# Convolution with max-pooling on one core: the last image pair's rows as bf16

## The chip, the cores and the metric

The kernel runs on one core of a Trainium2 chip. The metric is the time of one execution on the device, in microseconds (us); the lower the better. The core has five engines with instruction queues of their own: TensorE (PE, with its weight loads shown apart as PEld), VectorE (DVE), ScalarE (ACT), GpSimd (POOL) and SyncE (SP), which here only issues transfers. Matmul results go to PSUM (eight banks of 128 x 512 f32); all other operands lie in SBUF.

## The reference

A 3x3 convolution with padding 1 over 16 images of 64 channels and 64 x 64 points, to 128 output channels, then the maximum over 2x2 blocks:

```python
batch, c_in, h, w, c_out, k = 16, 64, 64, 64, 128, 3
...
x_pad = np.pad(x, ((0, 0), (0, 0), (pad, pad), (pad, pad)), mode='constant')
...
conv[b, co] += weight[co, ci, kh, kw] * x_pad[b, ci, kh:kh+h, kw:kw+w]
...
output[b, c, i, j] = np.max(conv[b, c, i*pool_size:(i+1)*pool_size,
                                      j*pool_size:(j+1)*pool_size])
```

Inputs and output are float32: x is (16, 64, 64, 64), the output (16, 128, 32, 32).

## The kernel before

**Tiling.** Two images lie one above the other on the 128 partitions (64 channels each), which makes eight pairs. Each pair is cut into four quarters of 16 image rows, so there are 32 steps, numbered 0 to 31. `SEQ` (line 14) gives each step its form: eight steps (pairs 0 and 1) are of the form K, 24 (pairs 2 to 7) of the form W. The last pair, 7, is steps 28, 29, 30 and 31, all W. A step's quarter makes 8 pairs of convolution rows, 8 x 64 = 512 columns, one PSUM bank per image and side. The two images of a pair are called lanes 0 and 1; their matmuls use one half of the array's rows each and are issued in turn, lane by lane (`flush`, line 515).

**What is multiplied.** Of two neighbouring convolution rows (sides A and B), which the pooling joins anyway, a W step computes four row products in place of six. It first forms rows from the loaded image: E, the difference of an even and an odd row (`re`, line 328), S, their sum (`rs`, line 310), and V, the differences of rows two apart (`rv`, line 338; `rv_half` at line 345 makes the even ones, Ve, and the odd ones, Vo, by themselves). E, S and V are written as bf16. The image rows that they read lie in `wx` as f32. The products are P2 (of E, into side A), P0 (of V, into A), P3 (of V, into B) and P1 (of S, into B). A K step reads rows cast to bf16 (`kx`) and forms one sum KS (line 304); its products are PAa, PAb, PBa, PBb and PR.

**What follows the products.** For a step and a lane: a seed copies A's first product into B's bank (SE on ACT, line 445; SEv on DVE, line 443); EV copies A's bank to SBUF on ACT (lines 429 and 431); MX takes the maximum of B and that copy on DVE, in place (line 449); then P1 (or PR) is added, which both sides share. OD copies the odd columns out on ACT (line 472), CM takes the maximum with the even ones on DVE (line 481), and ST stores the step.

**The order.** Nothing is scheduled by a program: `ORDER` (lines 16 to 80) is the order in which everything is issued, by hand, and each engine works through its own part of it in that order. A token names what is done, the step, the lane, and after the colon a bank or an engine (v for DVE, a for ACT, g for POOL): `E.28:v` is step 28's difference on DVE, `V.28:g` its row differences on POOL, `P2.28.1:1` its product P2 in lane 1, into bank 1.

**Loads.** `load` (line 258, token LX) brings a W step's rows into one of four f32 buffers `wx` (line 149), each for a whole pair, issued on SP's queue, behind `paced` (line 251): a load waits until the step 12 before it has left its last maximum. The stores wait in the same queue. `load_cast` (line 273, token LK) brings a K step's rows as bf16, by a DMA that casts and is issued on POOL's queue.

**Rows on DVE and POOL.** `row_op` (line 195) issues a row operation on an engine. If it is POOL, the operation is made to wait for the last row operation that was issued on DVE before it; operations issued on DVE set that mark (`last_row`). `lift` (line 287, token CP) copies a step's even rows into a PSUM bank on ACT; for a lifted step `two_rows` (line 292) forms E and S on DVE from that bank and from `wx`, and does not set the mark. Eleven steps are lifted, 28 and 30 among them. E, S and V of 29 and 31, and V of 28 and 30 (30's as halves), are formed on POOL.

```python
    def lift(s, bank):
        lifted[s] = acc[bank]
        nc.scalar.copy(out=acc[bank], in_=wrow(s, 0))
...
        if e == "v" and s in lifted:
            nc.vector.tensor_tensor(out=t, in0=lifted[s], in1=wrow(s, 1), op=op)
        else:
            row_op(e, t, wrow(s, 0), wrow(s, 1), op)
```

Of the kernel before, what the change touches and what calls it, by code (L numbers as in the profile page):

```python
# [63 lines left out]
LX.31 ST.17 P1.20.1 PBa.23.0:4 CM.24.1 OD.22.0 MX.24.0 SE.25.1:3 CM.22.0 EV.23.1 V.26:g SEv.25.0:2  # L64
P1.24.0 P0.25.1 OD.20.1 OD.24.0 EV.25.1 LX.30 ST.18 ST.22 ST.19 ST.21 PBb.23.0 P2.26.1:5 CM.20.1
ST.20 CM.24.0 ST.24 MX.23.0 SE.26.1:6 P3.25.1 P0.25.0 P3.25.0 PBa.23.1:0 EV.25.0 PR.23.0 P0.26.1
MX.25.1 P2.26.0:1 PBb.23.1 MX.25.0 E.29:g CP.28:7 S.26:g S.29:g E.28:v OD.23.0 P3.26.1 P1.25.0
V.28:g V.29:g CM.23.0 MX.23.1 Ve.30:g EV.26.1 P1.25.1 PAa.27.0:5 SE.26.0:4 PR.23.1 P0.26.0 MX.26.1
Ve.31:g P3.26.0 P1.26.1 Vo.30:g E.31:g OD.25.0 OD.25.1 EV.26.0 CM.25.0 S.28:v PAa.27.1:2 PAb.27.0
CP.30:7 CM.25.1 ST.25 MX.26.0 OD.23.1 P2.28.1:1 PBa.27.0:3 OD.26.1 PAb.27.1 P1.26.0 EV.27.0 CM.23.1  # L70
ST.23 PBb.27.0 PBa.27.1:0 CM.26.1 E.30:v SE.28.1:5 S.30:v Vo.31:g P0.28.1 P2.29.0:6 MX.27.0
P2.28.0:7 PBb.27.1 PR.27.0 P3.28.1 EV.27.1 OD.26.0 CM.26.0 ST.26 SE.29.0:2 MX.27.1 EV.28.1 OD.27.0
P2.29.1:4 P0.29.0 P3.29.0 PR.27.1 SE.28.0:1 EV.29.0 CM.27.0 MX.28.1 P0.28.0 P2.30.1:3 MX.29.0
# [10 lines left out]
def kernel(  # L84
# [7 lines left out]
    nc = tc.nc  # L92
    FP32 = mybir.dt.float32
    BF16 = mybir.dt.bfloat16
# [4 lines left out]
    B, CI, H, W = x.shape  # L99
# [4 lines left out]
    R = HO // NQ  # L104
# [3 lines left out]
    const = ctx.enter_context(tc.tile_pool(name="const", bufs=1))  # L108
# [16 lines left out]
    def behind(inst, other):  # L125
        if other is not None:
            tc.add_manual_dep(inst.ins, other.ins.name, SYNC, reason="order")
# [7 lines left out]
    def rows_of(p, lo, hi):  # L135
        return x[2 * p : 2 * p + 2].rearrange("b c h w -> (b c) h w")[:, lo:hi, :]

    def chunk(s):

        p, q = place[s]  # L140
        same = any(place[t] == (p, q - 1) and SEQ[t] == SEQ[s] for t in range(N))
        lo = 2 * R * q + 1 if same else max(0, 2 * R * q - 1)
        return p, lo, min(H, 2 * R * (q + 1) + 1)

    def half(s):
        return 2 * R * place[s][1] + R + 1

    NWX = 4
    wx = [const.tile([128, H + 2, W], FP32, name=f"wx_{i}") for i in range(NWX)]
    for t in wx:  # L150
        nc.gpsimd.memset(t[:, 0, :], 0.0)
        nc.gpsimd.memset(t[:, H + 1, :], 0.0)
    kx = {}

    def kx_of(p):
        if p not in kx:
            kx[p] = kx_pool.tile([128, H, W], BF16, name="kx")
        return kx[p]
# [10 lines left out]
    make_identity(nc, ident)  # L169
    zeros = const.tile([128, 512], BF16)  # L170
    begun = nc.gpsimd.memset(zeros, 0.0)
    wv = wraw.rearrange("a (c k) -> a k c", k=K * K)

    def ring(t, k):
# [20 lines left out]
    def row_op(e, out, in0, in1, op):  # L195
        inst = eng[e].tensor_tensor(out=out, in0=in0, in1=in1, op=op)  # L196
        if e == "g":
            behind(inst, last_row[0])
        else:
            last_row[0] = inst  # L200
# [50 lines left out]
    def paced(s, inst):  # L251

        for l in (0, 1):
            behind(inst, done.get((s - AHEAD[SEQ[s]], l)))
        if SEQ[s] == "K" and s < AHEAD["K"] and s not in kf:
            behind(inst, done["head"])

    def load(s, part, e):
        p, lo, hi = chunk(s)
        if SEQ[s] == "W":  # L260
            t = wx[p % NWX]
            paced(s, nc.sync.dma_start(out=t[:, lo + 1 : hi + 1, :], in_=rows_of(p, lo, hi)))
            return
        if s not in kf:
            kf[s] = const.tile([128, hi - lo, W], FP32, name=f"kf_{s}")
        a, b = {"": (lo, hi), "a": (lo, half(s)), "b": (half(s), hi)}[part]
        q = nc.scalar if e == "a" else nc.sync
        inst = q.dma_start(out=kf[s][:, a - lo : b - lo, :], in_=rows_of(p, a, b))
        paced(s, inst)
        if e == "a":  # L270
            behind(inst, begun)
# [15 lines left out]
# [5 lines that stand above are left out]
    def two_rows(s, t, e, op):  # L292
# [5 lines that stand above are left out]
    def wrow(s, a):  # L298

        p, q = place[s]  # L300
        f = 2 * R * q + a + 1
        return wx[p % NWX][:, f : f + 2 * R - 1 : 2, :]

    def ks(s, e):
        p, q = place[s]
# [32 lines left out]
    def rv(s, e):  # L338
        p, q = place[s]
        t = row["V", s] = v_pool.tile([128, 2 * R, W], BF16, name="wv")  # L340
        f = 2 * R * q
        u = wx[p % NWX]
        row_op(e, t, u[:, f + 2 : f + 2 + 2 * R, :], u[:, f : f + 2 * R, :], SUB)

    def rv_half(s, e, odd):

        p, q = place[s]
        t = row["V" + "eo"[odd], s] = vh_pool.tile([128, R, W], BF16, name="vh")
        f = 2 * R * q + odd
        u = wx[p % NWX]  # L350
        row_op(e, t, u[:, f + 2 : f + 1 + 2 * R : 2, :], u[:, f : f + 2 * R - 1 : 2, :], SUB)


# [168 lines left out]
    for token in ORDER.split():  # L522
# [22 lines left out]
        elif name == "TV":  # L545
            turn_out(args[0], at)
        elif name == "LX":
            load(int(args[0].rstrip("ab")), args[0].lstrip("0123456789"), at)
        elif name == "LK":
            load_cast(int(args[0]))  # L550
        elif name == "CP":
            lift(int(args[0]), int(at))
        elif name in ("XO", "XE"):
            to_bf16(int(args[0].rstrip("ab")), args[0].lstrip("0123456789"), int(name == "XO"), at)
        elif name == "E" and not args[0].isdigit():
            re_half(int(args[0][:-1]), args[0][-1], at)
        elif name in ("KS", "S", "E", "V"):
            f = rs_cast if name == "S" and int(args[0]) in ADDED else None
            (f or {"KS": ks, "S": rs, "E": re, "V": rv}[name])(int(args[0]), at)
        elif name in ("Ve", "Vo"):  # L560
            rv_half(int(args[0]), at, int(name == "Vo"))
        elif name == "SA":
            rs_add(int(args[0]))
        elif name == "ST":
            l, part = (int(args[1][0]), args[1][1:]) if len(args) > 1 else (None, "")
            store(int(args[0]), l, part, at)
        else:
            s = int(args[0])
            l, part = (int(args[1][0]), args[1][1:]) if len(args) > 1 else (None, "")
            if name in ("SE", "SEv"):  # L570
                bank["B", s, l] = int(at)
                seed(s, l, name[2:])
                continue
            if name in ("OD", "CM", "RM"):
                {"OD": odd, "CM": colmax, "RM": pairmax}[name](s, l, part)
            else:
                {"EV": evac, "MX": rowmax}[name](s, l)
# [36 lines left out]
```

## Time and profile before

| | us |
|---|---|
| three timed runs, median | 103.27 |
| lowest and highest | 103.05, 103.55 |
| the profiled execution, from its first to its last instruction | 101.5 |

The profiled execution is known by its span alone; it is not one of the three timed runs. The clock granted to TensorE was full (1.000) throughout. A row of the timeline gives start and length in us, engine, line, operation, output and inputs by the program's names, and how many like instructions were put together; in square brackets stands the idle time just before it and what ended it. Row names do not carry the step; it is found by counting along the order text. The transfers moved 24.07 MB, at a mean of 237 GB/s.

### The profile page before, as it was taken

To read this page: it belongs to the slowest core of one execution; us is meant where nothing else is said; L and a number is where in the kernel's file an instruction comes from. 1 tells how busy PE (TensorE), PEld (TensorE's weight loads), DVE (VectorE), ACT (ScalarE), POOL (GpSimd) and SP (SyncE) were. 2 spreads that over 40 slices of the span, in tenths; PEclk is the share of its full clock that TensorE was granted. 3 is DMA by queue.
4 is the path that set the end of the run, shared out by engine and by line. 5 is a ranking of instruction groups with operands and counts; after the bars stand their busy time and mean duration, and the time that the engine had idled before them with its cause. 6 is when DMAs were issued, how large, how long until landed. Compare 5 with 4: busy or idle time off the path is not lost.

```text
span 101.5 us, 2486 instructions
## 1 busy us (share of the span) xinstructions
PE 96.4 (95%) x870; PEld 55.6 (55%) x870; DVE 91.4 (90%) x181; ACT 89.5 (88%) x198; POOL 79.3 (78%) x65
## 2 busy tenths in 40 slices
PE   6999999999999999999989999999999999999950
PEld 2356885466666666555645555455475555655510
DVE  0599999999999999799999989998999999888980
ACT  5599999999988999998999989989989889899840
POOL 7000898988598599989999999998599999999000
PEclk9999999999999999999999999999999999999999
DMA  2999999991079989889998999999953915302353
GB/s 45 328 248 403 417 376 337 326 226 33 6 203 390 233 166 302 315 222 291 273 329 260 261 237 311 374 392 308 295 222 122 344 58 201 108 29 78 110 189 121
DMA packets 13789, 24.07 MB, mean 237 GB/s; under 512 B 1104, under 2 KB 9680, under 8 KB 13776
## 3 DMA queue, kind: packets, MB, share of 16 engines
q1 hardware_dynamic: 12624, 22.16, 64.9%
q0 software_dynamic: 864, 1.56, 10.2%
q10 hardware_dynamic: 288, 0.20, 0.6%
q8 instruction: 7, 0.11, 0.4%
q14 instruction: 6, 0.05, 0.1%
HBM read 17.07 MB, written 8.39 MB: 251 GB/s over the span
## 4 chain that ended last, share of the span: by engine, by line
PE 83%; ACT 6%; DVE 3%; DMA 3%; issue 2%; DVEq 0%; ACTq 0%
PE acc L414 80%; DMA wraw<-in_weight_dram 3%; ACT acc L445 3%; PE acc L229 2%; DVE acc L449 2%; ACT od L472 2%; ACT ev L429 1%; DVE o L481 1%; ACT wq L191 1%; DVE acc L443 0%; PE acc L439 0%; DVEq L609 0%; DVEq L449 0%; DVEq L443 0%; ACTq L290 0%
## 5 line engine op out<-in xcount | busy, mean ns | idle before, releaser
L414 PEld LDWEIGHTS <-wt 64*128 64x128 bf16 x840 | 52.8, 94 | 37.3 <-issue 2.5
L414 PE MATMUL acc<-wv,wt 64*128 64x504 bf16 (+1 forms) x228 | 49.5, 377 | 0.3 <-ACT acc L445 0.3
L449 DVE TENSOR_TENSOR acc<-acc,ev 128x512 f32<-128x512 f32 x64 | 42.9, 693 | 2.0 <-ACT ev L429 1.1
L196 POOL TENSOR_TENSOR wv<-wx 128x1024 bf16<-128x1024 f32 x18 | 42.3, 2362 | 2.5 <-DVE ks L196 1.6
L414 PE MATMUL acc<-kx,wt 64*128 64x504 bf16 (+6 forms) x216 | 38.9, 350 | 0.0
L414 PE MATMUL acc<-ws,wt 64*128 64x512 bf16 (+1 forms) x144 | 35.2, 377 | 0.2 <-DVE acc L449 0.2
L414 PE MATMUL acc<-we,wt 64*128 64x512 bf16 (+1 forms) x144 | 35.1, 377 | 0.0
L429 ACT ACTIVATE ev<-acc 128x512 f32<-128x512 f32 x48 | 28.6, 610 | 1.1 <-PE acc L414 1.0
L445 ACT COPY acc<-acc 128x512 f32<-128x512 f32 x45 | 26.3, 588 | 2.0 <-PE acc L414 0.4
L481 DVE TENSOR_TENSOR o<-acc,od 128x256 f32<-128x256 f32 (+1 forms) x65 | 25.7, 412 | 1.4 <-ACT od L472 0.5
L472 ACT COPY od<-acc 128x256 f32<-128x256 f32 x64 | 23.6, 382 | 2.7 <-PE acc L414 1.9
L196 POOL TENSOR_TENSOR we<-wx 128x512 bf16<-128x512 f32 x11 | 14.0, 1272 | 2.8 <-DVE ks L196 1.7
L414 PE MATMUL acc<-ks,wt 64*128 64x504 bf16 (+1 forms) x48 | 12.5, 377 | 0.0
L414 PE MATMUL acc<-vh,wt 64*128 64x504 bf16 (+1 forms) x60 | 10.4, 376 | 0.0
L196 POOL TENSOR_TENSOR ws<-wx 128x512 bf16<-128x512 f32 x8 | 10.1, 1268 | 0.1
L275 POOL DMA_DIRECT2D kx<-in_x_dram x6 | 3.5, 590 | 8.0 <-ACT ev L429 8.0
L431 ACT COPY ev<-acc 128x512 f32<-128x512 f32 x16 | 9.3, 598 | 0.4 <-PE acc L414 0.3
L196 POOL TENSOR_TENSOR vh<-wx 128x512 bf16<-128x512 f32 x7 | 8.8, 1272 | 0.5 <-DVE ks L196 0.4
L294 DVE TENSOR_TENSOR we<-acc,wx 128x512 bf16<-128x512 f32 x11 | 7.5, 682 | 0.0
L294 DVE TENSOR_TENSOR ws<-acc,wx 128x512 bf16<-128x512 f32 x11 | 7.5, 681 | 0.0
L290 ACT COPY acc<-wx 128x512 f32<-128x512 f32 x11 | 6.7, 607 | 0.1
L509 PE MATMUL acc<-const-bfloat16-1.0 128*128 128x512 bf16 x8 | 3.6, 625 | 0.8 <-PEq L595 0.8
(30 smaller groups left out, 34.3 us busy)
## 6 DMA issues: line engine op xcount, KB each, us to landing
out_dram<-o SPq DMA_DIRECT2D x30, 256.0 KB, 5.8
wx<-in_x_dram SPq DMA_DIRECT2D x12, 512.0 KB, 6.3
wx<-in_x_dram SPq DMA_DIRECT2D x6, 544.0 KB, 6.5
wx<-in_x_dram SPq DMA_DIRECT2D x6, 480.0 KB, 6.7
kx<-in_x_dram POOLq DMA_DIRECT2D x3, 256.0 KB, 7.2
kf<-in_x_dram SPq DMA_DIRECT2D x1, 512.0 KB, 7.7
kx<-in_x_dram POOLq DMA_DIRECT2D x2, 240.0 KB, 5.6
wraw<-in_weight_dram SPq DMA_DIRECT2D x1, 288.0 KB, 3.0
```

Source lines behind the costliest of these rows:

```text
L196: inst = eng[e].tensor_tensor(out=out, in0=in0, in1=in1, op=op)
L275: paced(s, nc.gpsimd.dma_start(out=kx_of(p)[:, lo:hi, :], in_=rows_of(p, lo, hi)))
L290: nc.scalar.copy(out=acc[bank], in_=wrow(s, 0))
L294: nc.vector.tensor_tensor(out=t, in0=lifted[s], in1=wrow(s, 1), op=op)
L414: yield lambda kw=kw, o0=o0, o1=o1, c0=c0, c1=c1: nc.tensor.matmul(acc[t][:, i0:i1, o0:o1], wt[l * CI : l * CI + CI, K * BLOCKS[block] + T ...
L429: inst = nc.scalar.mul(t, acc[bank["A", s, l]], -1.0)
L431: inst = nc.scalar.copy(out=t, in_=acc[bank["A", s, l]])
L445: nc.scalar.copy(out=acc[b], in_=acc[bank["A", s, l]])
L449: nc.vector.tensor_tensor(out=t, in0=t, in1=ev[s, l], op=MAX)
L472: nc.scalar.copy(out=od[s, l][:, i0:i1], in_=acc[bank["B", s, l]][:, i0:i1, 1::2])
L481: done[s, l] = nc.vector.tensor_tensor(out=outs(s)[:, l, i0:i1], in0=acc[bank["B", s, l]][:, i0:i1, 0::2], in1=od[s, l][:, i0:i1], op=MAX,)
L509: nc.tensor.matmul(acc[n], ones[:, 0:128], ones, start=True, stop=True, skip_group_check=True)
```

## The change

Pair 7 gets a buffer of its own, `hx`, in bf16. Its four loads (LX.28, LX.29, LX.31, LX.30) become casting DMAs, issued on POOL's queue at the places that the tokens have in the order; they have no pacing wait. All rows of steps 28 to 31 are read from `hx`. The tokens CP.28 and CP.30 are taken out, so E and S of these two steps are formed by `row_op` on DVE, from two operands in SBUF, and set the mark for which later row operations on POOL wait. POOL clears two border rows of `hx` at the start. The order is the same otherwise.

```diff
-MX.25.1 P2.26.0:1 PBb.23.1 MX.25.0 E.29:g CP.28:7 S.26:g S.29:g E.28:v OD.23.0 P3.26.1 P1.25.0
+MX.25.1 P2.26.0:1 PBb.23.1 MX.25.0 E.29:g S.26:g S.29:g E.28:v OD.23.0 P3.26.1 P1.25.0
...
-CP.30:7 CM.25.1 ST.25 MX.26.0 OD.23.1 P2.28.1:1 PBa.27.0:3 OD.26.1 PAb.27.1 P1.26.0 EV.27.0 CM.23.1
+ CM.25.1 ST.25 MX.26.0 OD.23.1 P2.28.1:1 PBa.27.0:3 OD.26.1 PAb.27.1 P1.26.0 EV.27.0 CM.23.1
...
+    HALF = B // 2 - 1
+    hx = const.tile([128, H + 2, W], BF16, name="hx")
+
+    def wx_of(p):
+        return hx if p == HALF else wx[p % NWX]
...
+    nc.gpsimd.memset(hx[:, 0, :], 0.0)
+    nc.gpsimd.memset(hx[:, H + 1, :], 0.0)
...
     def load(s, part, e):
         p, lo, hi = chunk(s)
         if SEQ[s] == "W":
-            t = wx[p % NWX]
+            t = wx_of(p)
+            if p == HALF:
+                nc.gpsimd.dma_start(out=t[:, lo + 1 : hi + 1, :], in_=rows_of(p, lo, hi))
+                return
             paced(s, nc.sync.dma_start(out=t[:, lo + 1 : hi + 1, :], in_=rows_of(p, lo, hi)))
             return
...
-        return wx[p % NWX][:, f : f + 2 * R - 1 : 2, :]
+        return wx_of(p)[:, f : f + 2 * R - 1 : 2, :]
...
-        u = wx[p % NWX]
+        u = wx_of(p)
```

The last pair of lines stands in `rv` and in `rv_half`.

More of the change, by code (lines that the diff above doesn't have):

```diff
@@ L349, in rv_half @@
         f = 2 * R * q + odd
-        u = wx[p % NWX]
+        u = wx_of(p)
         row_op(e, t, u[:, f + 2 : f + 1 + 2 * R : 2, :], u[:, f : f + 2 * R - 1 : 2, :], SUB)
```

## The prediction

> **What bounds the kernel now.** I read the shares of the page first, then the chain of waits, then the windows and the timeline of each engine. Busy shares and the chain by engine, from the page:
>
> ```profile
> PE 96.4 (95%) x870; PEld 55.6 (55%) x870; DVE 91.4 (90%) x181; ACT 89.5 (88%) x198; POOL 79.3 (78%) x65
> PE 83%; ACT 6%; DVE 3%; DMA 3%; issue 2%; DVEq 0%; ACTq 0%
> ```
>
> TensorE (PE) is the bound; DVE and ACT, at 90% and 88%, have little to give. In the chain in order of time (start, length, what), PE runs alone until 87.77; from there it hands over between ACT, DVE and PE to the end:
>
> ```profile
> 53.10 34.67 PE acc L414 x316
> 87.77 0.36 ACT od L472
> ...
> 95.69 0.71 DVE acc L449
> ...
> 96.44 1.41 PE acc L414 x6
> ```
>
> The last image pair (steps 28 to 31) is worked on from about 78 us. The window there shows POOL without a gap (8.00 of 8.00 us) beside a PE that is full too, and a light DMA (41%, 136 GB/s):
>
> ```profile
> 80.00:88.00 8.00, 8.00 (x78) 4.60 (x76) 7.74 (x16) 6.96 (x16) 8.00 (x6) 1.00 0.41 136
> ```
>
> The change adds work to that POOL. Its timeline (start, length), with the step each row is by the order text: V.24; E.26 after its wait; V.25 and V.26; E.29; S.26 and S.29; V.28 and V.29; Ve.30, Ve.31 and Vo.30; E.31.
>
> ```profile
> 68.44 2.35 POOL L196 TENSOR_TENSOR wv<-wx 128x1024 bf16<-128x1024 f32 x1
> 72.17 1.28 POOL L196 TENSOR_TENSOR we<-wx 128x512 bf16<-128x512 f32 x1 [1.38 <-DVE ks L196]
> 73.40 4.68 POOL L196 TENSOR_TENSOR wv<-wx 128x1024 bf16<-128x1024 f32 x2
> 78.04 1.27 POOL L196 TENSOR_TENSOR we<-wx 128x512 bf16<-128x512 f32 x1
> 79.27 2.50 POOL L196 TENSOR_TENSOR ws<-wx 128x512 bf16<-128x512 f32 x2
> 81.74 4.68 POOL L196 TENSOR_TENSOR wv<-wx 128x1024 bf16<-128x1024 f32 x2
> 86.38 3.73 POOL L196 TENSOR_TENSOR vh<-wx 128x512 bf16<-128x512 f32 x3
> 90.07 1.27 POOL L196 TENSOR_TENSOR we<-wx 128x512 bf16<-128x512 f32 x1
> ```
>
> Where PE takes these up, in its own timeline: PR.27.0, which follows MX.27.0 on DVE; P0.29.0, which reads V.29; P2.31, which reads E.31; and the weight-load row shows one wait on an ACT seed before P0.28.1.
>
> ```profile
> 86.92 0.38 PE L414 MATMUL acc<-ks,wt 64*128 64x512 bf16 x1
> 87.56 0.38 PE L414 MATMUL acc<-wv,wt 64*128 64x512 bf16 x1
> 92.08 0.83 PE L414 MATMUL acc<-we,wt 64*128 64x512 bf16 x6
> 85.57 6.20 PEld L414 LDWEIGHTS <-wt 64*128 64x128 bf16 x60 [0.23 <-ACT acc L445]
> ```
>
> So V.29 (done at 84.06 + 2.36 = 86.42, half of the row of two) is 1.14 us early and E.31 (done at 91.34) is 0.74 us early.
>
> **The change, part by part.** *Removed from ACT*: CP.28 and CP.30.
>
> ```profile
> 79.40 0.59 ACT L290 COPY acc<-wx 128x512 f32<-128x512 f32 x1
> 83.26 0.59 ACT L290 COPY acc<-wx 128x512 f32<-128x512 f32 x1
> 84.95 0.57 ACT L445 COPY acc<-acc 128x512 f32<-128x512 f32 x1
> ```
>
> That is 1.18 us of ACT, ahead of 87.77 where ACT enters the chain. At most SE.28.1 (84.95) comes earlier and the short wait of PE before 85.57 goes: a few tenths, and only if nothing else is late there. I count 0; bounds 0 to 0.6 us of gain.
>
> *Moved from SP to POOL*: the loads 28, 29, 31 and 30. POOL issues casting loads already:
>
> ```profile
> L275 POOL DMA_DIRECT2D kx<-in_x_dram x6 | 3.5, 590 | 8.0 <-ACT ev L429 8.0
> ```
>
> 0.59 us each. LX.28 and LX.29 fall before the 1.38 us wait ahead of E.26 and fit in it (1.18). LX.31 stands between V.25 and V.26, LX.30 behind V.26, with no gap to hide in: 2 x 0.59 = 1.18 us on all of POOL from E.29 on. SP loses four issues and their pacing waits, so the stores queued behind them can only go earlier; PE is busy there whatever SP does: 0. The two added clears of border rows come at the start, where POOL then idles (the 8.0 us of the same row): 0.
>
> *Landing.* POOL's casting loads landed, at the least and at the most:
>
> ```profile
> kx<-in_x_dram POOLq DMA_DIRECT2D x1, 240.0 KB, 5.2
> kx<-in_x_dram POOLq DMA_DIRECT2D x1, 256.0 KB, 7.9
> ```
>
> LX.30, the last, is issued at 73.40 + 4.64 + 0.16 + 0.59 = 78.8 (the 0.16 comes below) and lands between 84.0 and 86.7. Its first reader E.30 comes on DVE at 85.3; with the light DMA of that window I take the short end, no wait; the long end adds up to 0.8 us.
>
> *Four DVE operations now read two operands from SBUF*, where in0 came from PSUM. What that does beside a running POOL, the trace shows on the KS sums, which read SBUF twice in bf16:
>
> ```profile
> 28.11 2.37 POOL L196 TENSOR_TENSOR wv<-wx 128x1024 bf16<-128x1024 f32 x1 [1.23 <-DVE ks L196]
> 33.13 0.58 POOL L275 DMA_DIRECT2D kx<-in_x_dram  x1
> 39.52 4.67 POOL L196 TENSOR_TENSOR wv<-wx 128x1024 bf16<-128x1024 f32 x2
> 30.14 0.62 DVE L196 TENSOR_TENSOR ks<-kx 128x512 bf16<-128x512 bf16 x1
> 33.26 0.41 DVE L196 TENSOR_TENSOR ks<-kx 128x512 bf16<-128x512 bf16 x1
> 43.91 0.57 DVE L196 TENSOR_TENSOR ks<-kx 128x512 bf16<-128x512 bf16 x1
> ```
>
> Alone, or beside a DMA issue of POOL, a KS takes 0.41. Begun while a POOL subtraction runs it ends at 30.76 and 44.48, which is 0.28 after POOL's 30.48 and 44.19. So DVE stands until the POOL instruction is over and then needs its last 0.28 us. The DVE rows that matter: S.25, KS.27, E.28, S.28, E.30, S.30, MX.27.0:
>
> ```profile
> 71.08 0.68 DVE L196 TENSOR_TENSOR ws<-wx 128x512 bf16<-128x512 f32 x1
> 71.68 0.42 DVE L196 TENSOR_TENSOR ks<-kx 128x512 bf16<-128x512 bf16 x1
> 80.08 0.69 DVE L294 TENSOR_TENSOR we<-acc,wx 128x512 bf16<-128x512 f32 x1
> 82.55 0.68 DVE L294 TENSOR_TENSOR ws<-acc,wx 128x512 bf16<-128x512 f32 x1
> 84.86 0.68 DVE L294 TENSOR_TENSOR we<-acc,wx 128x512 bf16<-128x512 f32 x1
> 85.45 0.68 DVE L294 TENSOR_TENSOR ws<-acc,wx 128x512 bf16<-128x512 f32 x1
> 86.05 0.69 DVE L449 TENSOR_TENSOR acc<-acc,ev 128x512 f32<-128x512 f32 x1
> ```
>
> The four at L294, with one operand in PSUM, took an even 0.68 to 0.69 beside a busy POOL. As bf16 they would be 0.42 like KS, 0.26 less each, if POOL were still.
>
> The walk. LX.28 pushes V.24's end from 70.79 to 71.38, so S.25 (71.08) stands 0.3 and ends 0.16 late; E.26, which waits for KS.27 behind it, likewise. E.29 starts at 78.04 + 0.16 + 1.18 = 79.38 and ends 80.65; E.28 (80.24) ends at 80.93, no later than before. I let POOL's next instruction give way 0.28 for each DVE operation (no row shows this; bounds 0 and 0.42). S.29 then ends at 83.39: S.28 ends at 83.67 in place of 83.23, DVE +0.44. V.28 ends at 86.00: E.30 ends at 86.28, DVE +0.74. Now S.30 and V.29 both want the operands. If V.29 goes first it ends at 88.60 and S.30 at 88.88, 2.75 late; MX.27.0 right behind it, and PR.27.0 on PE, are late by the same 2.75. If S.30 goes first, DVE is only 0.49 late, but V.29 ends at 88.94, 1.4 after P0.29.0 wanted it at 87.56, and E.31 at 93.80, 1.7 after P2.31's 92.08: PE +1.8 with the hand-over. No row decides between the two; I take the middle, +2.25.
>
> [...]
>
> *POOL's own subtractions in bf16*: ten of them, 8 x 1.27 + 2 x 2.36 = 14.9 us. No row has POOL read bf16. The nearest are DVE's pair 0.68 to 0.42 (0.62 times) and, upward, a conversion against a plain copy on ACT, 0.646 to 0.59 (1.09 times):
>
> ```profile
> L191 ACT CAST kx<-kf 128x512 bf16<-128x512 f32 x2 | 1.2, 646 | 0.0
> ```
>
> I take unchanged, since POOL's rows cost the elements and its output was bf16 already; the ends are 5.7 us less and 1.3 more.
>
> **Sum.** Against the profiled span of 101.5: -0 (ACT), +2.25: 103.75. The runs' median is 1.8 above that span, so 103.27 + 2.25 = 105.5 us.
>
> **The rivals.** *POOL keeps the operands over back-to-back instructions.* For it: in every clash above the next POOL instruction waited for the DVE one by order (the [1.23 <-DVE ks]), so no row shows DVE getting in between two. E.28 would wait for S.29 (V.28 waits for E.28), S.28 for everything up to E.31, as only Vo.31 waits for the DVE row ahead of it: 83.4 + 9.6 + 0.3 = 93.3 in place of 83.2, +10: 113 us. Against: the rows show separate instructions, each with its end.
>
> *No clash, only the issues.* If bf16 rows of this size pass beside POOL, just the 1.34 us of delay stay: V.29 ends at 87.8, E.31 at 92.7, PE +0.65: 103.9. Against: the KS rows.
>
> *Faster: POOL becomes short.* At 0.62 times on eight of the ten it has read (E.29, S.29, V.28, V.29 first), the two late issues are caught up before V.28 and the clashes are short. It decides at V.29 over before E.30's 84.86: 7.26 r + 1.27 must fit in 84.86 - 79.38 = 5.48, so r below 0.58. Then ACT's 1.18 and DVE's 4 x 0.26 us count, of which the few tenths at 85.57 and half a microsecond behind 87.77 reach the end: about 102.5. For it: half the bytes. Against: that POOL's time must nearly halve; between 0.58 and 0.75 gain and clash cancel, 103.2.
>
> **How the numbers follow.** Half a per cent, 0.52 us, is about what these runs (103.05 to 103.55) can tell from no change. Chances: the forecast 0.62 (own range 104.3 to 107.0, by its two branches, the late landing and POOL's dearer end), POOL keeping on 0.10, issues alone 0.10, cancelling 0.05, faster 0.13. Range 102.6 to 108.0: it leaves out the 113 case and the far end of the faster one. Slower by over 0.5%: 0.80, the three cases above with a little taken off for the smallest; within 0.07; faster 0.13.
>
> **What would show it.** Right: E.28, S.28, E.30 or S.30 on DVE longer than 0.42 and each ending some 0.28 after a POOL row; PE idle ahead of PR.27.0 or P0.29.0; two 0.59 us issues between V.25 and E.29; E.29 on POOL near 79.4. Wrong: those four rows at an even 0.42, POOL rows on hx well under 1.27, or E.30 released by a DMA and not by POOL.

## The result and the profile after

| | before | changed |
|---|---|---|
| time, median of four executions each, us | 103.41 | 107.72 |
| lowest and highest, us | 103.05, 103.78 | 106.61, 114.0 |
| profiled execution: span, and its own time, us | 101.5, not timed | 106.1, 107.92 |

The changed kernel takes 1.0372 times as long (95% interval 1.0306 to 1.0438). The execution of 114.0 us is not in that ratio; it stands for a second way in which the kernel runs, and a profile of that kind is read below (changed_again).

The page of the changed kernel: busy shares, the granted clock in 40 slices, the chain by engine.

```profile
PE 98.3 (93%) x870; PEld 55.8 (53%) x870; DVE 95.0 (90%) x181; ACT 88.5 (83%) x196; POOL 80.9 (76%) x71
PEclk9999999999999999999999999999999958999998
PE 58%; ACT 16%; DVE 10%; DMA 6%; issue 5%; SPq 1%; DVEq 0%; ACTq 0%
```

PE's part of the chain fell from 83% to 58%, and two slices between 85 and 90 us show TensorE at 0.5 and 0.8 of its full clock. The windows of the changed kernel say where (window, length, busy time of PE, PEld, DVE, ACT and POOL, clock, DMA):

```profile
80.00:84.00 4.00, 2.15 (x20) 1.00 (x17) 4.00 (x4) 1.12 (x3) 3.54 (x4) 1.00 0.98 235
84.00:88.00 4.00, 3.68 (x20) 2.13 (x21) 3.34 (x8) 2.12 (x6) 4.00 (x3) 0.59 0.56 177
```

From 80 to 84 us PE worked 2.15 of 4 us, and DVE was busy for all 4 with four instructions. From 84 to 88 the clock was 0.59. Its DVE and POOL timelines around there, and the PE rows that follow:

```profile
80.25 3.07 DVE L203 TENSOR_TENSOR we<-hx 128x512 bf16<-128x512 bf16 x1
83.25 0.41 DVE L491 TENSOR_TENSOR o<-acc,od 128x256 f32<-128x256 f32 x1
83.58 1.28 DVE L459 TENSOR_TENSOR acc<-acc,ev 128x512 f32<-128x512 f32 x2
...
85.11 0.79 DVE L203 TENSOR_TENSOR ws<-hx 128x512 bf16<-128x512 bf16 x1
...
86.89 0.70 DVE L459 TENSOR_TENSOR acc<-acc,ev 128x512 f32<-128x512 f32 x1 [0.66 <-ACT od L482]
...
88.17 1.11 DVE L203 TENSOR_TENSOR we<-hx 128x512 bf16<-128x512 bf16 x1
89.20 1.38 DVE L203 TENSOR_TENSOR ws<-hx 128x512 bf16<-128x512 bf16 x1
90.50 0.69 DVE L459 TENSOR_TENSOR acc<-acc,ev 128x512 f32<-128x512 f32 x1
```

```profile
78.95 0.58 POOL L270 DMA_DIRECT2D hx<-in_x_dram  x1
79.55 1.17 POOL L203 TENSOR_TENSOR we<-hx 128x512 bf16<-128x512 bf16 x1
80.67 1.26 POOL L203 TENSOR_TENSOR ws<-wx 128x512 bf16<-128x512 f32 x1
81.89 1.14 POOL L203 TENSOR_TENSOR ws<-hx 128x512 bf16<-128x512 bf16 x1
83.49 4.39 POOL L203 TENSOR_TENSOR wv<-hx 128x1024 bf16<-128x1024 bf16 x2 [0.46 <-DVE we L203]
87.84 3.74 POOL L203 TENSOR_TENSOR vh<-hx 128x512 bf16<-128x512 bf16 x3
```

```profile
84.32 0.37 PE L424 MATMUL acc<-ks,wt 64*128 64x512 bf16 x1 [2.17 <-DVE acc L459]
...
85.22 0.63 PE L424 MATMUL acc<-ws,wt 64*128 64x512 bf16 x1
...
91.24 0.37 PE L424 MATMUL acc<-ks,wt 64*128 64x512 bf16 x1
```

E.28 took 3.07 us on DVE. It ended at 83.32, 0.29 behind the end of S.29 on POOL (81.89 + 1.14 = 83.03): it stood not only for E.29, which was running when it began, but for S.26 and S.29 as well. MX.23.1 came late behind it, and PE waited 2.17 us for it before PR.23.1. Then a matmul took 0.63 in place of 0.38, as the clock was at 0.50 up to about 88. Counted along PE by the starts of its products: PR.23.0 is 0.2 us late (79.37 in place of 79.17), PR.23.1 behind the wait 2.54 (84.32 in place of 81.78), and the products from there up to PR.27.0 take 1.8 us more than before, nearly all of it at the lower clock. PR.27.0 is then 4.32 late (91.24 in place of 86.92), and so are the last products (100.76 in place of 96.44).

Counted along DVE the same stretch reads otherwise. MX.27.0, which PR.27.0 waits for, is 4.45 us late (90.50 in place of 86.05): 2.56 by E.28, 0.13 by S.28, 0.62 by the wait ahead of 86.89 (MX.26.0 reads what P3.26.0 wrote, which ended on PE at 86.80), 0.44 by E.30 and 0.70 by S.30. MX.27.0 ends at 91.19 and PR.27.0 starts at 91.24. By these rows PE at full clock would have come earlier and waited there, so its 1.7 us at the lower clock are not simply time lost at the end. Along DVE the clock enters by the 0.62, and no run shows which POOL instruction an earlier E.30 would have met.

### The profile page after: what moved, and what is told of

It is laid out like the page before. It is cut to its first block, busy times and chain, and to the rows that moved or that the text cites. A ratio compares the mean times of both kernels' runs of the same rounds, so it can differ in the third digit from the quotient of the medians.

```text
span 106.1 us, 2487 instructions
## 1 busy us (share of the span) xinstructions
PE 98.3 (93%) x870; PEld 55.8 (53%) x870; DVE 95.0 (90%) x181; ACT 88.5 (83%) x196; POOL 80.9 (76%) x71
## 4 chain that ended last, share of the span: by engine, by line
PE 58%; ACT 16%; DVE 10%; DMA 6%; issue 5%; SPq 1%; DVEq 0%; ACTq 0%
PE acc L424 57%; ACT acc L455 6%; DVE acc L459 6%; ACT ev L439 4%; DMA out_dram<-o 3%; ACT od L482 3%; DMA wraw<-in_weight_dram 3%; DVE o L491 2%; ACT wt L247 2%; PE acc L236 1%; DVE ws L304 1%; SPq L514 1%; DVE acc L453 1%; ACT wq L198 1%; ACT ev L441 1%
## 5 line engine op out<-in xcount | busy, mean ns | idle before, releaser
L424 PE MATMUL acc<-wv,wt 64*128 64x504 bf16 (+1 forms) x228 | 50.5, 382 | 0.3 <-ACT acc L455 0.3
L424 PE MATMUL acc<-kx,wt 64*128 64x504 bf16 (+7 forms) x216 | 39.6, 357 | 0.1
L203 POOL TENSOR_TENSOR wv<-wx 128x1024 bf16<-128x1024 f32 x16 | 37.7, 2362 | 2.6 <-DVE ks L203 1.6
L203 POOL TENSOR_TENSOR we<-wx 128x512 bf16<-128x512 f32 x9 | 11.5, 1276 | 1.9 <-DVE ws L203 1.0
L203 POOL TENSOR_TENSOR ws<-wx 128x512 bf16<-128x512 f32 x6 | 7.6, 1267 | 0.1
L304 DVE TENSOR_TENSOR ws<-acc,wx 128x512 bf16<-128x512 f32 x9 | 6.1, 680 | 0.0
L304 DVE TENSOR_TENSOR we<-acc,wx 128x512 bf16<-128x512 f32 x9 | 6.1, 680 | 0.0
L300 ACT COPY acc<-wx 128x512 f32<-128x512 f32 x9 | 5.5, 612 | 0.1
L203 POOL TENSOR_TENSOR vh<-hx 128x512 bf16<-128x512 bf16 x4 | 4.9, 1246 | 0.0
L203 POOL TENSOR_TENSOR wv<-hx 128x1024 bf16<-128x1024 bf16 x2 | 4.4, 2218 | 0.5 <-DVE we L203 0.5
```

What stands on the lines that cost most here:

```text
L424: yield lambda kw=kw, o0=o0, o1=o1, c0=c0, c1=c1: nc.tensor.matmul(acc[t][:, i0:i1, o0:o1], wt[l * CI : l * CI + CI, K * BLOCKS[block] + T ...
```

## The experiments

Medians are given beside those of the kernel before, timed along with them on the same chip, with the ratio and its 95% interval.

**lifts_back: the copies into PSUM put back, loads as changed.**

```diff
-... MX.25.0 E.29:g S.26:g S.29:g E.28:v ...
+... MX.25.0 E.29:g CP.28:7 S.26:g S.29:g E.28:v ...
...
- CM.25.1 ST.25 MX.26.0 ...
+CP.30:7 CM.25.1 ST.25 MX.26.0 ...
```

> Keeps the bf16 buffer and the casting loads on POOL's queue, and puts the two copies into PSUM back (steps 28 and 30), so that DVE reads one operand of E and S from SBUF again. Theory (DVE stands while POOL's back-to-back instructions hold the shared operand path, here 3.07 us in E.28): E.28 back at 0.68, no wait of PE for PR.23.1, clock full throughout, 103.3 to 104.0 us; what is left over 103.4 is the price of four issues on POOL. Rival (the loads do it, by their issue or landing on POOL's queue): stays above 106.

106.66 us (before 103.34), ratio 1.0244, 1.0178 to 1.0311. The theory was only half right: E and S were back at 0.68 or 0.69 each, but the time, above 106, was the rival's. The rows show how long DVE stood, 3.07 us in the changed kernel beside 0.69 here; that POOL then holds a shared operand path is the author's reading, which no row shows. ACT's timeline, and the DMA view of load 30:

```profile
86.63 0.59 ACT L300 CAST acc<-hx 128x512 f32<-128x512 bf16 x1 [2.77 <-DMA hx<-in_x_dram]
```

```profile
hx<-in_x_dram POOLq DMA_DIRECT2D x1, 256.0 KB, 7.2
```

CP.30 is wanted at 83.86 and had to wait 2.77 us for load 30, which was issued at 79.36 and took 7.2 us to land. ACT, PE and DVE stood behind it. In the changed kernel this second cause is covered by the first: E.30 came so late there that load 30 had landed.

**f32_no_lift: the kernel before, without the two copies.**

```diff
-... E.29:g CP.28:7 S.26:g ...
+... E.29:g S.26:g ...
...
-CP.30:7 CM.25.1 ST.25 ...
+ CM.25.1 ST.25 ...
```

> The kernel before with nothing changed but the two copies into PSUM dropped; loads and rows stay f32 and on SP. Theory (two operands from SBUF beside POOL): slower like the changed kernel, 105.5 to 109 us, with E.28, S.28, E.30 or S.30 longer than 0.68 and ending some 0.54 after a POOL row; if POOL in f32 never lets DVE in between two of its instructions, S.28 waits for all of V.28 to E.31 and the time is about 113. Rival (bf16 rows or the moved loads are needed for the loss): 103.0 to 103.5.

106.77 us (103.34), ratio 1.0316, 1.028 to 1.0352: dropping the copies alone costs 3.4 us, without bf16 rows and without any load moved. DVE's and POOL's timelines of it:

```profile
80.46 1.05 DVE L196 TENSOR_TENSOR we<-wx 128x512 bf16<-128x512 f32 x1
...
83.29 2.21 DVE L196 TENSOR_TENSOR ws<-wx 128x512 bf16<-128x512 f32 x1
...
87.02 1.25 DVE L196 TENSOR_TENSOR we<-wx 128x512 bf16<-128x512 f32 x1
88.19 1.75 DVE L196 TENSOR_TENSOR ws<-wx 128x512 bf16<-128x512 f32 x1
```

```profile
79.69 2.94 POOL L196 TENSOR_TENSOR ws<-wx 128x512 bf16<-128x512 f32 x2
82.59 5.12 POOL L196 TENSOR_TENSOR wv<-wx 128x1024 bf16<-128x1024 f32 x2
```

The four take 6.26 us together, where they took 2.73 in the kernel before: 3.5 more, about the whole loss. Every stand ends 0.55 behind the POOL instruction that was running, and the next POOL instruction pays too: the pair S.26 and S.29 takes 2.94 in place of 2.50, V.28 and V.29 5.12 in place of 4.68, 0.44 more each. All four executions lay within 106.62 to 106.96.

**e28_first: E.28 ahead of S.26 and S.29 in the order.**

```diff
-... E.29:g S.26:g S.29:g E.28:v ...
+... E.29:g E.28:v S.26:g S.29:g ...
```

> The changed kernel with E.28 put ahead of S.26 and S.29 in the order, so that POOL's S.26 waits for E.28 and DVE has only E.29 to wait for. Theory (the 2.17 us wait of PE, and the half clock behind it, come from E.28 standing behind S.26 and S.29 as well): E.28 ends near 81.1 in place of 83.3, PR.23.1 waits 0.2 at most, clock full; 104.0 to 105.0 us, the rest from S.28, E.30 and S.30. Rival (the order of these rows does not matter, DVE is late for another reason): within 0.7 of the changed kernel, 107.

106.62 us (103.34), ratio 1.0288, 1.024 to 1.0336: the long stand of E.28 went, but the time stayed above the 104.0 to 105.0 expected. DVE's and PE's timelines:

```profile
79.81 0.74 DVE L203 TENSOR_TENSOR we<-hx 128x512 bf16<-128x512 bf16 x1
...
82.34 0.97 DVE L203 TENSOR_TENSOR ws<-hx 128x512 bf16<-128x512 bf16 x1
...
85.37 2.28 DVE L203 TENSOR_TENSOR we<-hx 128x512 bf16<-128x512 bf16 x1 [0.47 <-DMA hx<-in_x_dram]
87.57 1.36 DVE L203 TENSOR_TENSOR ws<-hx 128x512 bf16<-128x512 bf16 x1
88.86 0.68 DVE L459 TENSOR_TENSOR acc<-acc,ev 128x512 f32<-128x512 f32 x1
```

```profile
89.59 0.37 PE L424 MATMUL acc<-ks,wt 64*128 64x512 bf16 x1 [2.59 <-DVE acc L459]
```

With DVE on time, E.30 meets load 30 on its way: it waits 0.47 for the landing, begins just after V.29 has (85.25 on POOL) and stands for the whole of it, 2.28 us. MX.27.0 starts at 88.86 in place of 86.05, and PE waits 2.59 us before PR.27.0. Freed in one place, most of the loss came back in the next.

**pe_filled and pe_filled_again: matmuls on zeros in the stretch where PE waits.**

```diff
-... SE.26.0:4 PR.23.1 P0.26.0 ...
+... SE.26.0:4 FILL.10:7 PR.23.1 P0.26.0 ...
...
+        if name == "FILL":
+            for _ in range(int(args[0])):
+                nc.tensor.matmul(
+                    acc[int(at)], zeros[:, 0:128], zeros, start=True, stop=True, skip_group_check=True
+                )
```

> The changed kernel with ten matmuls on zeros, into the bank that the dropped copy left free, ahead of PR.23.1: work that nothing reads, 10 x 0.22 us, in the stretch in which PE waits. Theory (part of the loss is the clock: PE at 0.50 for 3.3 us after a wait of 2.2 us, which costs 1.6): clock 1.00 throughout, E.28 as late as before, 105.8 to 106.4 us. Rival (the lower clock is no result of the wait, or costs nothing since DVE sets the pace there): 107.5 or above.

> The kernel with ten matmuls on zeros ahead of PR.23.1 once more, for a profile of an execution near its median of 106.6. Theory: clock 1.00 in 84 to 88 us as long as DVE's stand is under some 3 us; PR.23.1 waits for MX.23.1 as before, for what the filling leaves. Rival: the clock falls to 0.50 behind that wait all the same.

106.64 us (103.34), ratio 1.0299, 1.026 to 1.0338. That is a microsecond under the changed kernel, but the two intervals overlap, and neither profile fell on an execution near the median: they took 113.88 and 114.0 us, with S.28 on DVE for 8.08 us in both. What the low clock costs by itself is therefore not shown, nor is the bound of some 3 us on DVE's stand that the second expectation gives. In e28_first a wait of 2.59 us passed with the clock at 1.00.

**changed_again: the changed kernel, a second profile.**

> The changed kernel as it is, for a second profile. Theory: whether DVE gets in between two back-to-back POOL instructions differs from execution to execution, so the four stands of E.28, S.28, E.30 and S.30 are not the same lengths as in the first profile (3.07, 0.79, 1.10, 1.37), and the time follows them: 106 to 108, or about 114 where S.28 stands until E.31 is over. Rival (the stands are fixed by the order): the same four lengths within 0.2 and 107.5 to 108.

114.91 us. Its DVE and POOL timelines, and the window:

```profile
80.04 2.08 DVE L203 TENSOR_TENSOR we<-hx 128x512 bf16<-128x512 bf16 x1
...
83.90 8.08 DVE L203 TENSOR_TENSOR ws<-hx 128x512 bf16<-128x512 bf16 x1
```

```profile
80.47 1.27 POOL L203 TENSOR_TENSOR ws<-wx 128x512 bf16<-128x512 f32 x1
81.69 1.43 POOL L203 TENSOR_TENSOR ws<-hx 128x512 bf16<-128x512 bf16 x1
83.08 4.19 POOL L203 TENSOR_TENSOR wv<-hx 128x1024 bf16<-128x1024 bf16 x2
87.24 3.34 POOL L203 TENSOR_TENSOR vh<-hx 128x512 bf16<-128x512 bf16 x3
90.55 1.14 POOL L203 TENSOR_TENSOR we<-hx 128x512 bf16<-128x512 bf16 x1
94.31 1.15 POOL L203 TENSOR_TENSOR vh<-hx 128x512 bf16<-128x512 bf16 x1 [2.62 <-DVE ws L203]
```

```profile
88.00:92.00 4.00, 0.00 (x0) 0.00 (x0) 4.00 (x2) 0.00 (x0) 3.69 (x4) 0.50 0.00 0
```

S.28 stood while POOL ran six subtractions, from V.28 to E.31, and ended 0.29 behind the last (91.69). POOL stopped behind E.31 because Vo.31 waits by order for S.30, which stands behind S.28 on DVE. E.28 took 2.08: it ended 0.38 behind S.26 (81.74), so it lost to E.29 and S.26 and got in ahead of S.29's end, without a wait of POOL. PE and ACT did nothing from 88 to 92 us. So the stands are not fixed by the order: the same program had 3.07 and 0.79 for E.28 and S.28 in the first profile, 2.08 and 8.08 in this one.

**loads_early and early_and_lifts: the casting loads issued 45 to 51 us sooner, without and with the copies.**

```diff
-... OD.3.0 V.7:g EV.4.1 ...
+... OD.3.0 V.7:g LX.28 LX.29 EV.4.1 ...
-... V.10:g E.10:g MX.4.1 ...
+... V.10:g E.10:g LX.31 LX.30 MX.4.1 ...
```

The four tokens are taken out where they stood; early_and_lifts has CP.28 and CP.30 back besides.

> The changed kernel with the four casting loads issued early on POOL's queue: 28 and 29 behind V.7, 31 and 30 behind E.10, near 22 and 27 us, where POOL has waits of 0.71 and 1.23 us and the DMA is nearly idle. No copies into PSUM. Theory (two causes that hide each other: DVE standing behind POOL, and load 30 landing late): with the loads gone from the end only the first is left, and since each alone costs over 2 us, 105.2 to 106.8. Rival (the late loads are the larger part): 103.3 to 104.5.

> The same early loads, and the two copies into PSUM put back: both suspected causes taken away, with the bf16 buffer and the casting loads kept. Theory: level with the kernel before, 102.9 to 103.6; POOL's ten subtractions on bf16 take 1.15 and 2.12 us and are done earlier than before, which nothing waits for. Rival (casting loads or bf16 rows cost something of their own): 104.5 or more.

loads_early 105.3 us (103.37), ratio 1.0183, 1.0143 to 1.0224. early_and_lifts 103.87 us (103.37), ratio 1.0045, 1.0024 to 1.0065, over twelve executions. With both causes taken away all but half a microsecond of the loss is gone (the expectation was 102.9 to 103.6); with the loads alone out of the way the clashes stay. In bf16 they cost 1.4 us (105.3 beside 103.87), against 3.4 in f32; the other 2.4 us of the changed kernel (107.72 less 105.3) came with the places of its loads. DVE's timeline of loads_early, with the longest two:

```profile
82.67 1.60 DVE L203 TENSOR_TENSOR ws<-hx 128x512 bf16<-128x512 bf16 x1
...
86.45 1.37 DVE L203 TENSOR_TENSOR ws<-hx 128x512 bf16<-128x512 bf16 x1
```

In early_and_lifts the chain of waits is again PE from the middle to the last maxima:

```profile
53.42 42.47 PE acc L424 x388
```

Its half microsecond over the kernel before is not explained; in the profile 0.2 to 0.3 us of it stands at the start, ahead of the first products, and as much behind the last instruction of DVE.

**no_copy_28 and no_copy_30: one copy dropped at a time, loads early.**

```diff
 no_copy_28 (early_and_lifts without CP.28)
-... E.29:g CP.28:7 S.26:g ...
+... E.29:g S.26:g ...
 no_copy_30 (early_and_lifts without CP.30)
-CP.30:7 CM.25.1 ...
+ CM.25.1 ...
```

> Early loads, the copy of step 30 kept and that of step 28 dropped: of the four clashes E.28 and S.28 are left. Theory: S.28 is late by half a microsecond to one, behind which MX.26.0 and two maxima stand with some slack; 103.6 to 104.6 us. Rival (the first stands are the costly ones): as with both copies dropped, 105.0 or more.

> Early loads, the copy of step 28 kept and that of step 30 dropped: E.30 and S.30 are left, with MX.27.0 and so PR.27.0 right behind them. Theory: E.30 or S.30 stands behind V.29 for up to 2.1 us and PE waits for all of it; 104.6 to 106.0 us, more than with only the copy of step 28 dropped. Rival (the two pairs cost alike, or the stands are hidden there): 104.2 or less.

104.75 us, ratio 1.013 (1.009 to 1.017), and 104.78 us, ratio 1.0125 (1.0099 to 1.0151), both beside 103.53. Each pair of clashes costs about 0.9 us over early_and_lifts; that step 30 would be the dearer, as expected, did not hold, and the first was 0.15 above its range.

**one_load_no_wait and one_load_then_wait: one casting load ahead of the clash.** Both are loads_early with load 31 moved: ahead of E.29, from where POOL goes on back to back, or ahead of E.26, in front of which POOL stands waiting.

```diff
-... MX.25.0 E.29:g S.26:g ...
+... MX.25.0 LX.31 E.29:g S.26:g ...
 and in the other
-... MX.22.0 E.26:g
+... MX.22.0 LX.31 E.26:g
```

> Both copies into PSUM dropped, three casting loads early, and load 31 alone issued on POOL right ahead of E.29, from where POOL works back to back without a wait up to V.28. Its data are first needed at about 86. Theory (behind the issue of a casting load POOL's back-to-back instructions leave DVE no gap, until POOL itself has stood waiting once; this is why E.28 stood 3.07 us and S.28 8.08): E.28 or S.28 stands across several POOL instructions in the profile, and the executions spread, 106 to 114 us, some of them near 113. Rival (the long stands came by chance, or from load 30's landing): as with all loads early, 104.9 to 106.1, each stand over with the POOL instruction that was running.

> The same, with load 31 issued on POOL ahead of E.26, where POOL then waits some 0.8 us for KS.27 before it goes on. Theory (the wait behind the issue ends the trouble): as with all loads early, 104.9 to 106.1 us in every execution, each stand over with the POOL instruction that was running. Rival (any casting load in this stretch is enough): spread up to 114 as without the wait.

106.44 us (ratio 1.0272, 1.0227 to 1.0317; six executions from 105.82 to 107.61) and 105.03 us (1.0156, 1.0119 to 1.0194; six from 105.02 to 105.49), beside 103.46. DVE and POOL of the first:

```profile
80.30 2.36 DVE L203 TENSOR_TENSOR we<-hx 128x512 bf16<-128x512 bf16 x1
```

```profile
78.28 0.58 POOL L270 DMA_DIRECT2D hx<-in_x_dram  x1
78.87 1.17 POOL L203 TENSOR_TENSOR we<-hx 128x512 bf16<-128x512 bf16 x1
79.99 1.26 POOL L203 TENSOR_TENSOR ws<-wx 128x512 bf16<-128x512 f32 x1
81.22 1.14 POOL L203 TENSOR_TENSOR ws<-hx 128x512 bf16<-128x512 bf16 x1
82.82 4.39 POOL L203 TENSOR_TENSOR wv<-hx 128x1024 bf16<-128x1024 bf16 x2 [0.46 <-DVE we L203]
```

E.28 began while S.26 ran (to 81.25) and still ended 0.30 behind S.29 (82.36). Then V.28 waited for it, 0.46 us, and from there on each stand was over with one POOL instruction. In the other kernel, POOL and DVE:

```profile
72.28 1.26 POOL L203 TENSOR_TENSOR we<-wx 128x512 bf16<-128x512 f32 x1 [0.84 <-DVE ks L203]
```

```profile
80.14 0.68 DVE L203 TENSOR_TENSOR we<-hx 128x512 bf16<-128x512 bf16 x1
```

The same load, with 0.84 us of waiting on POOL before the back-to-back stretch, and E.28 took 0.68. The second kernel stayed within its 104.9 to 106.1. For the first the expected long stand came, the executions near 113 did not.

Two other readings have to be set against this one. A load still on its way is not enough: in e28_first S.28 stood behind S.29 alone (82.34 to 83.31) while load 30 had not landed, and in changed_again S.28 stood on to 91.98, long after load 30, issued at 78.76, had landed (6.5 us later). The two kernels here differ also in where E.28 falls on POOL's row, 0.31 us into S.26 in the first and 0.86 in the other. An early start is not enough by itself: S.30 of loads_early began 0.24 into Ve.30 (86.45 and 86.21) and was over with it. But no run moved the start alone, and there is one profile of each of these kernels.

## Why the prediction was right, and where it was not

**The mechanism was right.** The forecast put the loss into four DVE operations that stand while POOL subtracts, and f32_no_lift shows it by itself: the dropped copies cost 3.4 us with nothing else changed. In bf16 the stands ended 0.28 to 0.30 behind a POOL row, as the KS rows of before had shown (0.38 for E.28 in changed_again). A profile of the changed kernel also shows the two 0.58 us issues between V.25 and E.29, and E.29 at 79.55 where 79.38 was worked out.

**The number was in part luck.** 107.72 lies outside the range that the forecast's two branches gave (104.3 to 107.0) and 0.3 us inside the outer one. What the branches describe, each stand over with one POOL instruction, is loads_early, at 1.9 us over the kernel before; the rest came from long stands that the forecast had as a rival, and one of four executions took the 114 us that the range left out.

**The step that failed is that each stand ends with the POOL instruction that was running: "DVE stands until the POOL instruction is over", after which "I let POOL's next instruction give way 0.28".** E.28 was to end at 80.93, behind E.29 alone; it ended at 83.32, behind three, and put the wait of PE at PR.23.1 and not at PR.27.0 or P0.29.0. The rival "POOL keeps the operands over back-to-back instructions" was worked out to 93.3 for S.28's end and 113 us; the second profile of the changed kernel shows 91.98 and 114.91. That rival, given 0.10, is thus a part of what happens: at E.28 in both profiles of the changed kernel, at S.28 in one. The two kernels with one moved load point to what brings it on: a casting load issued on POOL with no wait of POOL behind it. Without such a load (f32_no_lift, loads_early, no_copy_28, no_copy_30) DVE got in at the next boundary, in the one profile of each: its longest stands were 2.21 us in the first and 1.60 in the second, and PE waited for it 0.4 and 0.9 us at the longest in the other two. So the trigger is supported but not proven, for the reasons given there. In e28_first the load is there, but POOL waits 0.37 us for E.28 right behind E.29, and again each later stand was over with one instruction.

**The clock was not foreseen.** The forecast's sum of +2.25 had no term for it. In the first profile it took 1.7 us of PE's time, but along DVE, whose MX.27.0 released PR.27.0, it shows only in the wait of 0.62. What it cost at the end is open: the filling matmuls did not settle it, and e28_first lost 3.3 us with the clock at 1.00 throughout. The low stretch here (0.84 from 84 to 85 us, 0.50 up to 88, 0.95 up to 89) followed a wait of PE of 2.17 us; none followed the one of 2.59 in e28_first. What sets it off, no run shows.

**The landing was mis-sized.** "The short end, no wait" is right for the changed kernel only because E.30 was late itself. Load 30 took 7.2 us where ACT was on time (lifts_back), and E.30 waited 0.47 for it in e28_first: the long end of the range, 7.9, came nearer. The light DMA of 80 to 88 us, from which the short end was taken, was not light any more: its share is 0.98 from 80 to 84 us, against 0.43 before.

**S.30 or V.29 first** was met in another place: E.30 stood behind V.29 in e28_first, and the price was MX.27.0 late by 2.81, where the branch had 2.75. In the changed kernel Ve.30 and Ve.31 were in the way, 0.7 and 1.0 us.

**Smaller terms.** POOL's subtractions on bf16 were taken as unchanged; undisturbed they take 1.14 and 2.11 us in place of 1.27 and 2.36 (the rows of `hx` in lifts_back, least, median and most in ns):

```profile
L203 POOL TENSOR_TENSOR vh<-hx x4: 1139/1142/1145, 87.6 to 92.0; 128x512 bf16<-128x512 bf16 x4
L203 POOL TENSOR_TENSOR wv<-hx x2: 2107/2112/2117, 83.4 to 85.5; 128x1024 bf16<-128x1024 bf16 x2
```

That is 0.9 times, well above the 0.58 at which the faster case was to begin. That POOL's rows cost the elements was the author's reading of f32 rows alone (1.27 us for 512 columns, 2.36 for 1024); here half the bytes read took 0.9 of the time. The 1.18 us taken from ACT brought nothing that could be seen. The DVE row at 71.08 that the prediction calls S.25 is S.24; its stand was there (0.91 against 0.68). What put PE back by 0.2 us at 71 us was V.24 itself, later on POOL behind LX.28: P0.24.1, which reads it, started at 71.58, right behind its end at 71.53. The forecast had no term for that. The 1.23 that the prediction quotes for the rival is the wait ahead of the POOL row at 28.11; behind the two clashes POOL waited 0.36 us each, so the argument stands.

**No version beat the kernel before.** The nearest, early_and_lifts, is 0.45% slower.

## What to carry to other kernels

Before an operand is moved out of PSUM on DVE, look at what POOL does in that stretch: here a bf16 operation of 0.42 us with two operands in SBUF cost the rest of POOL's instruction (E and S of steps 28 and 30 took 0.68 to 2.28 us where they stood behind one), and at worst that of the whole row of instructions behind it (3.07 behind three, 8.08 behind six). A copy on another engine that looks like waste (0.59 us here) can be what keeps two engines apart: without the two of them f32_no_lift took 3.4 us longer. When loads move to a queue that an engine also computes on, give that engine a wait behind the issue, or issue them where it waits anyway (105.03 us in one_load_then_wait, 106.44 in one_load_no_wait), and work out anew when they land (7.2 us for load 30 in lifts_back); two late causes can hide each other, so undo both before judging either.

## What the runs showed of the hardware

- DVE lost to POOL not once but several times in a row: 2.36 us (one_load_no_wait), 3.07 (the changed kernel) and 8.08 (changed_again) for an operation that took 0.41 while POOL waited (E.30 and S.30 in changed_again, at 93.49 and 93.83). In the profiles this came behind a casting load issued on POOL, and these three ended when POOL stood waiting (0.46, 0.46 and 2.62 us seen); the 2.08 of changed_again ended without. Why DVE did not get in between two POOL instructions there, no run shows.
- Where DVE got in, POOL's next instruction paid for it: 0.44 us in f32 (f32_no_lift: S.26 and S.29 2.94 us, 2.50 before), some 0.2 in bf16 (V.28 and V.29 4.39 us in the first profile of the changed kernel, 4.19 in changed_again, where DVE did not get in).
